# Hybrid decoder layer on one core: output projection with its weight differences in 2 KB buffers, two of the four and the last branch's merge on VectorE, and low parts ordered behind the state additions

## The chip, the core and the metric

The kernel runs on one core of a Trainium2 chip. The core has five engines, each with an instruction queue of its own that is worked off in order: TensorE (PE in the profile; its weight loads are listed as PEld), VectorE (DVE), ScalarE (ACT), GpSimd (POOL) and SyncE (SP). SP does no arithmetic; it issues nearly all DMA transfers. POOL can issue DMAs too, and only there does this kernel use a DMA that adds to its destination. An engine waits on semaphores, so an instruction at the head of a queue that waits holds everything queued behind it.

The metric is the time of one execution on the device, in microseconds (us). Smaller is better. The time before is the median of three runs.

## The reference

One layer of a decoder trunk over 1024 tokens of width 1024, in float32. Three branches (sparse attention, a convolution module, cross-attention into a memory) are projected to the model's width, merged by gates, and sent through one output projection `w_out`. A gated MLP follows.

```python
merged = gm[:, :, 0] * br_nsa + gm[:, :, 1] * br_conv + gm[:, :, 2] * br_mem
h = x + merged @ w_out

hn = rms_norm(h, norm_ffn)
return h + (jax.nn.silu(hn @ w_gate) * (hn @ w_up)) @ w_down
```

Each `gm` is the sigmoid of a projection of the normed input, each `br` a branch times its own output weight (512 by 1024). The change touches the last steps of `merged` and the product `merged @ w_out`, with the addition of `x`.

## The kernel before

**Number format.** A float32 operand of a product is split in a high part (a copy to the type `float32r`) and a low part (the operand minus its high part). A product takes three matmuls per tile of 128 rows: high by high, high by low, low by high. `split` (L134) makes the parts. ScalarE always writes the high part (L135). The low part is a subtraction on VectorE (`sub`, L127; the instruction shows as L128), or on GpSimd when that engine is passed. If `nc.sync` is passed, ScalarE writes minus the high part into the low part's place (L138) and an adding DMA from GpSimd's queue adds the operand (L139).

**Buffers.** `slab` has 16 buffers of 8 KB per partition. Weight parts come from `wsl` (3) and `fsl` (2); `anyslab` deals them out in the fixed turn wsl, wsl, fsl, wsl, fsl. Raw loads land in `st` (2 buffers of 4 KB), `t4` (4 of 4 KB) or `t2` (6 of 2 KB); the profile writes tiles of both `t4` and `t2` as `t`. There are eight PSUM banks of 128x512: three each of two pools, one of a third (all `ps`) and one `pf`.

**The merge (L872 to L912).** Branches are handled in the order convolution, memory, attention (`n_` = 0, 1, 2). Each makes 16 products of 128 channels by 512 tokens, 12 matmuls each. For each 128 channels `d_`, the raw gates are loaded into a `t4` tile `zz` (L883), made a sigmoid by ScalarE (L884), and for each half of the tokens VectorE multiplies PSUM by the gates (L895 for the first branch, L897 for the others). From the second branch on, GpSimd adds the result to the sum in `acc` (L898). In the last branch three of the four quarters of the sum are split at once into `left` (L904; 12 of the 16 products), and `a_sums` (L864) makes four combinations of the quarters on VectorE, one call for each pair of channel groups.

**The output projection (L1042 to L1097).** The product of 1024x1024 by 1024x1024 is made as seven half-size products (a Strassen-Winograd scheme). Products are collected in two sets of four PSUM banks, `X` and `Y`; each is 48 matmuls (`out_product`, L1024, matmuls at L1031). After some of them `into_h` (L1034) adds the banks to the state `H` on VectorE (L1038) and, for a final piece, ScalarE sums its squares (L1040). A product that starts a set anew, or goes on with it, must wait until `into_h` has read the bank. The order is:

1. `X` = `left[0,0]` by `w_1`, where `w_1` is the first quarter B11 of the weight; into H.
2. `Y` = `s_1` by `w_5`, with `w_5` the parts of B12-B11; into H.
3. `X` += `s_2` by `w_6`, with `w_6` the parts of B22-(B12-B11); into H.
4. `Y` += `s_4` by `w_3` (B22), one row tile after the other; into H, final.
5. `Y` = `left[0,1]` by `w_2` (B21), by tile; into H, final.
6. `X` += `s_3` by `w_7` (B22-B12) and `left[1,1]` by `w_4` (B21 minus the difference used for `w_6`), in two groups of two row tiles, each followed by an `into_h` (in `finish`), while the state is normed and transposed for the MLP (L959 to L1012).

The weight differences are kept in `t_`, two `t4` tiles of 128 x 2 x 512, from L910 until `w_4` has been split (L1078); GpSimd works them out at L912, L1052 and L1064, and the ones for `w_7` at L1072. The quarters B11, B22, B21 and the minuend of `w_7` pass through the two `st` buffers one after another, so each load waits for the users of the one before. `w_1`, `w_5`, `w_6` and `w_3` use the adding DMA for their low parts; `w_2`, `w_7` and `w_4` use VectorE.

The state `H` (four slabs of 1 MB) is loaded from `x` by SP at L1045, after the parts of `s_1` in program order.

**What sets the order.** The kernel is written as one stream. The framework puts each engine's instructions in an order when the program is built, by priority in program order and by a simulated timeline of its own (`schedule_with_timeline_sim=True`, L1314). On the chip that order is fixed; what differs from the simulated times becomes waiting. `tc.add_manual_dep` with `ORDER` (L32, used by `behind`, L130) adds an edge that orders two instructions in the queue without a semaphore.

Of the kernel before, what the change touches and what calls it, by code (L numbers as in the profile page):

```python
# [8 lines left out]
F32 = mybir.dt.float32  # L9
# [3 lines left out]
OP = mybir.AluOpType  # L13
# [26 lines left out]
def hybrid_layer_kernel(  # L40
# [4 lines left out]
    nc = tc.nc  # L45
# [40 lines left out]
    def t4(shape, dt=F32):  # L86
        return t4p.tile([P] + shape, dt, tag="t4", name=nm("t4"))

    def t2(shape, dt=F32, p=P):
        return t2p.tile([p] + shape, dt, tag="t2", name=nm("t2"))  # L90
# [34 lines left out]
            tc.cur_priority = self.was  # L125

    def sub(eng, o, a, b):  # L127
        eng.tensor_tensor(o, a, b, op=OP.subtract)  # L128

    def behind(m, before, reason):  # L130
        for b in before or ():
            tc.add_manual_dep(m.ins, b.name, ORDER, reason=reason)

    def split(hi, lo, src, eng=None, after=None):  # L134
        first = nc.scalar.copy(hi, src)  # L135
        behind(first, after, "behind the parts of the rows")
        if eng is nc.sync:
            nc.scalar.activation(lo, hi.bitcast(F32), AF.Copy, scale=-1.0)  # L138
            nc.gpsimd.dma_start(lo, src, accum_op=OP.add)  # L139
        else:  # L140
            sub(eng or nc.vector, lo, src, hi.bitcast(F32))
        return first.ins

    def recip_rms(ss, n, eps, w):
# [191 lines left out]
    sums = []  # L336
# [48 lines left out]
    b = bank([4, TAPS + 3])  # L385
# [5 lines left out]
    b = bank([2, 16])  # L391
# [45 lines left out]
    b = bank([NT, 24])  # L437
# [75 lines left out]
    for hp in range(2):  # L513
# [3 lines left out]
        b = bank([2, 256])  # L517
# [3 lines left out]
        hi, lo = (KM[:, hl, 2 * hp:2 * hp + 2, :] for hl in range(2))  # L521
# [90 lines left out]
    with low(TAP):  # L612
        along = products[first_tap:]
        total, run, j = sum(n for _, n in along), 0, 0
# [200 lines left out]
    with low(FILL):  # L815
        for n_ in range(3 * KT):
            b_, d_ = n_ // KT, n_ % KT
            w = w_first if n_ == 0 else col_unit(w_in, C_GM + b_ * D + d_ * P, alloc=fslab,
                                                 eng=nc.sync if n_ > 2 else nc.gpsimd)
            for h_ in range(2):  # L820
                ps = fbank([512])
                for k in range(KT):
                    first = mm3(ps, w[:, 0, k, :], w[:, 1, k, :], xn(0, k, h_), xn(1, k, h_), k == 0, k == KT - 1)
                    j = ((n_ - N_EARLY) * 2 + h_) * KT + k
# [14 lines left out]
    def w_src(kh, dh, j):  # L839
        r0 = (4 * kh + 2 * j) * P  # L840
        return w_out[r0:r0 + 256, halves[dh]].rearrange("(k p) c -> p k c", p=P)

    def w_load(kh, dh, alloc):
        ts = [alloc() for _ in range(2)]
        for j, t in enumerate(ts):
            nc.sync.dma_start(t, w_src(kh, dh, j))
        return ts
# [1 line left out]
    def st2():  # L849
        return stage.tile([P, 2, 512], F32, tag="st", name=nm("st"))  # L850

    def w_parts(ts, eng=None):
        ws = [anyslab([2, 2, 512]) for _ in ts]
        for w, t in zip(ws, ts):
            split(w[:, 0], w[:, 1], t, eng)
        return ws

    def a_parts(th, kh):
        a = [slab([2, 2, 512]) for _ in range(2)]
        for j in range(2):  # L860
            split(a[j][:, 0], a[j][:, 1], merged(th, kh, j))
        return a
# [11 lines left out]
    for n_, (br, src, wt) in enumerate(branches):  # L874
        ins = nxt
        for dp in (range(4) if n_ < 2 else (0, 2, 1, 3)):
            w = unit(wt[0, :, dp * 256:(dp + 1) * 256].rearrange("(k p) c -> p k c", p=P), [4, 256], alloc=anyslab)
            if dp == 2 and n_ < 2:
                nxt = [unit(branches[n_ + 1][1][k], [S], alloc=slab) for k in range(4)]
            for d_ in (2 * dp, 2 * dp + 1):  # L880
                wc = (d_ % 2) * P
                zz = t4([S])
                nc.sync.dma_start(zz, zd[br, d_])  # L883
                nc.scalar.activation(zz, zz, AF.Sigmoid)  # L884
                for half in range(2):
                    z = zz[:, half * 512:(half + 1) * 512]
                    ps = anybank([512])
                    for k in range(4):
                        i_ = ins[k]
                        mm3(ps, w[:, 0, k, wc:wc + P], w[:, 1, k, wc:wc + P],  # L890
                            i_[:, 0, half * 512:(half + 1) * 512], i_[:, 1, half * 512:(half + 1) * 512],
                            k == 0, k == 3)
                    a = acc[dp][:, d_ % 2, half * 512:(half + 1) * 512]
                    if n_ == 0:
                        nc.vector.tensor_tensor(a, ps, z, op=OP.mult)  # L895
                    else:
                        nc.vector.tensor_tensor(z, ps, z, op=OP.mult)  # L897
                        nc.gpsimd.tensor_tensor(a, a, z, op=OP.add)  # L898
                    if n_ == 2 and (half, dp // 2) != (1, 0):
                        m = left.setdefault((half, dp // 2), [None, None])  # L900
                        if d_ % 2 == 0:
                            m[dp % 2] = slab([2, 2, 512])
                        m = m[dp % 2]
                        split(m[:, 0, d_ % 2, :], m[:, 1, d_ % 2, :], a)  # L904
            if n_ == 2 and dp > 1:
                a_sums(dp - 2)
            if n_ == 2 and dp == 1:
                b11 = w_load(0, 0, st2)
                w_1 = w_parts(b11, nc.sync)
                t_ = w_load(0, 1, lambda: t4([2, 512]))  # L910
                for t, b in zip(t_, b11):
                    sub(nc.gpsimd, t, t, b)  # L912

    hd = drp.tile([4, P, 2, D], F32, tag="hd", name="hd")
    FH = FF // P // 2
# [118 lines left out]
    def into_h(B, th, dh, final, ts=range(4)):  # L1034
        for t in ts:
            tp, tt = 2 * th + t // 2, t % 2
            h = H[tp][:, tt, cols[dh]]
            nc.vector.tensor_tensor(h, B[t], h, op=OP.add)  # L1038
            if final:
                nc.scalar.activation(junk, h, AF.Square, accum_out=sq4[tp][:, 2 * tt + dh:2 * tt + dh + 1])  # L1040

    s_1 = a_parts(1, 1)  # L1042
    for tp in range(4):
        H[tp] = slab([2, D], F32)
        nc.sync.dma_start(H[tp], x[tp * 256:(tp + 1) * 256, :].rearrange("(t p) d -> p t d", p=P))  # L1045
    w_5 = w_parts(t_, nc.sync)
    out_product(X, left[0, 0], w_1, True)
    into_h(X, 0, 0, False)
    s_2 = a_parts(0, 0)
    b22 = w_load(1, 1, st2)  # L1050
    for t, b in zip(t_, b22):
        sub(nc.gpsimd, t, b, t)  # L1052
    w_6 = w_parts(t_, nc.sync)
    out_product(Y, s_1, w_5, True)
    into_h(Y, 1, 1, False)
    s_4 = a_parts(0, 1)
    w_3 = w_parts(b22, nc.sync)
    out_product(X, s_2, w_6, False)
    into_h(X, 0, 1, False)
    s_3 = a_parts(1, 0)  # L1060
    b21 = w_load(1, 0, st2)
    w_2 = w_parts(b21)
    for t, b in zip(t_, b21):
        sub(nc.gpsimd, t, b, t)  # L1064
    out_product(Y, s_4, w_3, False, by_tile=True)
    into_h(Y, 0, 1, True)
    w_7 = []
    for j in range(2):
        t, b = st2(), t4([2, 512])
        nc.sync.dma_start(t, w_src(1, 1, j))  # L1070
        nc.sync.dma_start(b, w_src(0, 1, j))
        sub(nc.gpsimd, t, t, b)  # L1072
        w_7 += w_parts([t])
    out_product(Y, left[0, 1], w_2, True, by_tile=True)
    into_h(Y, 0, 0, True)
    for tp in range(2):
        nc.sync.dma_start(hd[tp], H[tp])
    w_4 = w_parts(t_)  # L1078
    def finish(tp, a, w, dh):
        ts = range(2 * (tp - 2), 2 * (tp - 1))  # L1080
        out_product(X, a, w, False, by_tile=True, ts=ts)
# [88 lines left out]
    w = pieces(1)  # L1170
# [147 lines left out]
```

## Time and profile before

| | |
|---|---|
| time, median of 3 runs | 1721.66 us (1720.76 to 1721.7) |
| time of the profiled execution | 1721.86 us |
| span in its profile | 1720.2 us, 24513 instructions |
| busy: PE, DVE, ACT, POOL | 98%, 61%, 46%, 34% |
| mean granted TensorE clock | 0.995 |

The profiled execution lies 1.66 us above its span: that is what lies around the span. Start times in the profile are microseconds from the span's start. A row of the timeline gives start, length, engine, line, operation, output and input tiles and the count of merged instructions; in brackets stands idle time of the engine before it and what ended it. The last products of the merge run on PE until about 984 us, the output projection from there to about 1096 us, and the MLP from there to the end.

### The profile page before, as it was taken

What the parts mean: (1) busy time and instruction counts of PE and PEld (TensorE: products, weight loads), DVE (VectorE), ACT (ScalarE), POOL (GpSimd) and SP (SyncE); (2) the same over time, 40 slices, a digit from 0 to 9 for tenths busy, and PEclk for the clock granted to TensorE, in tenths of its full rate; (3) what the DMA queues carried; (4) which work ended last, traced back from release to release, by engine and by line L of the source; (5) the groups of instructions that cost most, each with busy time, mean ns of one, the idle gap of its engine ahead of it and who ended that gap; (6) DMA issues with size and microseconds to landing.
All of it is one profiled execution on the core that took longest, in us unless ns stands there. A gap on an engine that the chain in (4) does not pass through costs nothing.

```text
span 1720.2 us, 24513 instructions
## 1 busy us (share of the span) xinstructions
PE 1686.9 (98%) x9050; PEld 1452.6 (84%) x9050; DVE 1051.3 (61%) x1773; ACT 789.0 (46%) x1427; POOL 588.6 (34%) x549
## 2 busy tenths in 40 slices
PE   7999999999999999999999988999999999999999
PEld 7887898999888889989888877888888888888887
DVE  5399798644355456766754677865455544457655
ACT  6413655534476566766654345532222232233332
POOL 1101012323254334343205731665565777310000
PEclk9999999999999999999999999999999999999999
DMA  6435445243233322121475563232333454794663
GB/s 198 108 79 153 121 123 125 61 106 99 74 92 88 91 69 59 50 70 57 131 249 195 141 202 135 80 123 90 113 98 116 147 166 165 266 374 155 227 233 122
DMA packets 180673, 230.12 MB, mean 134 GB/s; under 512 B 11382, under 2 KB 118056, under 8 KB 179530
## 3 DMA queue, kind: packets, MB, share of 16 engines
q1 hardware_dynamic: 173786, 203.92, 35.7%
q0 software_dynamic: 6768, 24.64, 7.6%
q8 instruction: 71, 1.16, 0.3%
q14 instruction: 48, 0.39, 0.1%
HBM read 153.55 MB, written 50.33 MB: 119 GB/s over the span
## 4 chain that ended last, share of the span: by engine, by line
PE 90%; DMA 3%; ACT 2%; DVE 2%; issue 1%; POOL 1%; SPq 0%; POOLq 0%; DVEq 0%; ACTq 0%
PE ps L154 52%; PE pf L154 18%; PE ps L1252 11%; PE ps L776 3%; PE ps L1031 2%; PE pf L1252 1%; DMA st<-in_w_out_dram 1%; DMA wsl<-st 1%; PE ps L220 1%; POOL t L128 0%; POOL slab L898 0%; ACT slab L135 0%; DMA t<-in_w_out_dram 0%; DMA wsl<-in_cmp_w_dram 0%; PE ps L702 0%
## 5 line engine op out<-in xcount | busy, mean ns | idle before, releaser
L154 PE MATMUL ps<-slab,wsl 128*128 128x512 f32 (+1 forms) x1616 | 360.5, 381 | 0.4 <-DMA wsl<-in_cmp_w_dram 0.4
L154 PEld LDWEIGHTS ps<-slab,wsl 128*128 128x128 f32 x1616 | 293.4, 188 | 58.4 <-issue 0.5
L154 PE MATMUL pf<-slab,fsl 128*128 128x512 f32 x1236 | 327.0, 401 | 3.9 <-ACT fz L828 3.8
L154 PEld LDWEIGHTS pf<-slab,fsl 128*128 128x128 f32 x1236 | 223.5, 189 | 44.9 <-ACT fz L828 5.3
L154 PE MATMUL ps<-wsl,slab 128*128 128x256 f32 x1344 | 173.2, 285 | 0.3 <-DVE slab L229 0.2
L154 PEld LDWEIGHTS ps<-wsl,slab 128*128 128x128 f32 x1344 | 167.4, 192 | 3.1 <-issue 1.0
L1150 DVE TENSOR_TENSOR t<-ps,t 128x512 f32<-128x512 f32 x127 | 86.8, 687 | 120.2 <-PE ps L154 119.4
L154 PE MATMUL ps<-slab,fsl 128*128 128x512 f32 x684 | 159.5, 389 | 0.0
L404 DVE SCALAR_TENSOR_TENSOR slab<-slab,cw 128x1021 f32<-128x1021 f32 (+15 forms) x120 | 156.0, 1303 | 2.2
L154 PEld LDWEIGHTS ps<-slab,fsl 128*128 128x128 f32 x684 | 128.4, 188 | 26.7
L128 DVE TENSOR_TENSOR t<-ps,t 128x512 fp32r<-128x512 f32 (+3 forms) x195 | 119.5, 630 | 31.6 <-ACT t L135 30.2
L135 ACT CAST t<-ps 128x512 fp32r<-128x512 f32 (+2 forms) x192 | 98.1, 539 | 44.5 <-PE ps L776 34.9
L1252 PE MATMUL ps<-wsl 128*128 128x512 f32 x492 | 117.7, 389 | 0.0
L154 PE MATMUL ps<-t,slab 128*128 128x256 f32 x624 | 116.4, 291 | 1.2 <-DVE t L128 1.2
L1252 PEld LDWEIGHTS ps<-wsl 128*128 128x128 f32 x492 | 92.3, 188 | 19.2
L135 ACT CAST wsl<-st 128x1024 fp32r<-128x1024 f32 x64 | 67.2, 1050 | 80.1 <-PE ps L154 34.5
L154 PEld LDWEIGHTS ps<-t,slab 128*128 128x128 f32 x624 | 94.2, 189 | 7.6 <-DVE t L128 1.6
L154 PE MATMUL ps<-slab,qt 128*128 128x384 f32 (+3 forms) x384 | 95.2, 339 | 1.0 <-DVE sm L744 1.0
L135 ACT CAST wsl<-t 128x1024 fp32r<-128x1024 f32 x45 | 47.4, 1054 | 96.5 <-POOL t L128 32.9
L690 POOL TENSOR_SCALAR wsl<-wsl,sm,gsb 128x640 f32<-128x640 f32 (+7 forms) x76 | 59.0, 791 | 87.0 <-DVE sm L685 82.7
L1252 PE MATMUL ps<-fsl 128*128 128x512 f32 x333 | 80.5, 389 | 0.0
L1163 POOL TENSOR_TENSOR t<-t,t 128x512 f32<-128x512 f32 x21 | 40.2, 1913 | 116.8 <-DVE t L1150 53.7
(256 smaller groups left out, 2858.8 us busy)
## 6 DMA issues: line engine op xcount, KB each, us to landing
t<-in_w_down_dram SPq DMA_DIRECT2D x70, 256.0 KB, 3.7
fst<-in_w_in_dram SPq DMA_DIRECT2D x24, 512.0 KB, 4.5
zd<-fz SPq DMA_DIRECT2D x48, 256.0 KB, 2.3
t<-zd SPq DMA_DIRECT2D x24, 512.0 KB, 4.7
st<-in_w_in_dram SPq DMA_DIRECT2D x22, 512.0 KB, 4.7
st<-in_w_gate_dram SPq DMA_DIRECT2D x22, 512.0 KB, 3.9
st<-in_w_up_dram SPq DMA_DIRECT2D x22, 512.0 KB, 4.1
ad<-t SPq DMA_DIRECT2D x44, 256.0 KB, 2.7
```

Source lines behind the costliest of these rows:

```text
L128: eng.tensor_tensor(o, a, b, op=OP.subtract)
L135: first = nc.scalar.copy(hi, src)
L154: m = nc.tensor.matmul(o, a, b, start=start, stop=stop)
L220: m = nc.tensor.transpose(b[:, kk, tt * P:(tt + 1) * P], js[tt][:, k * P:(k + 1) * P], ident)
L404: return nc.vector.scalar_tensor_tensor(acc[:, s:], u[:, :S - s], cw[:, ct, 30 - s:31 - s], acc[:, s:], op0=OP.mult, op1=OP.add)
L690: nc.gpsimd.tensor_scalar(tiles[h], tiles[h], rec[:, h:h + 1], gsb[:, i, c0:c0 + 1], op0=OP.mult, op1=OP.mult)
L776: nc.tensor.transpose(b[:, j - j0, h, :], tiles[h][:, j * P:(j + 1) * P], ident)
L1031: nc.tensor.matmul(B[t], a_, b_, start=start and k == 0 and j == 0, stop=k == 3 and j == 2, skip_group_check=True)
L1150: nc.vector.tensor_tensor(o, a_, b_, op=OP.add)
L1163: nc.gpsimd.tensor_tensor(u4, u4, c22, op=OP.mult)
L1252: nc.tensor.matmul(B[t], a_, b_, start=start and k == 0 and j == 0, stop=k == FH - 1 and j == 2, skip_group_check=True)
```

## The change

The diff is shown whole but for the context that it leaves alone.

- `split` and `w_parts` take `low_after`: instructions behind which the low part's subtraction is ordered on its engine. `into_h` returns its last addition for this. So `w_2`'s low parts are ordered behind the additions of product 3, `w_7`'s behind those of product 4, `w_4`'s behind those of product 5.
- `t_` becomes four `t2` tiles of 128x512 instead of two `t4` tiles of 128x1024. It is loaded by four DMAs instead of two, and its parts for `w_5`, `w_6` and `w_4` are made in pieces of 512 columns: twice the ScalarE instructions, and twice the adding DMAs or VectorE subtractions, each half as wide. `w_sums` makes the differences in the same pieces.
- The differences at L1064 and L1072 (for `w_4` and `w_7`) go from GpSimd to VectorE; those at L912 and L1052 (for `w_5` and `w_6`) stay on GpSimd.
- The additions at L898 go to VectorE in the last branch.
- The loads of `H[0]` and `H[1]` stand ahead of `s_1`'s parts in the program.

```diff
     def sub(eng, o, a, b):
-        eng.tensor_tensor(o, a, b, op=OP.subtract)
+        return eng.tensor_tensor(o, a, b, op=OP.subtract)
...
-    def split(hi, lo, src, eng=None, after=None):
+    def split(hi, lo, src, eng=None, after=None, low_after=None):
...
-            sub(eng or nc.vector, lo, src, hi.bitcast(F32))
+            behind(sub(eng or nc.vector, lo, src, hi.bitcast(F32)), low_after, "behind the sums of the blocks before")
...
-    def w_parts(ts, eng=None):
+    def w_parts(ts, eng=None, low_after=None):
         ws = [anyslab([2, 2, 512]) for _ in ts]
         for w, t in zip(ws, ts):
-            split(w[:, 0], w[:, 1], t, eng)
+            if isinstance(t, list):
+                for k in range(2):
+                    split(w[:, 0, k], w[:, 1, k], t[k], eng, low_after=low_after)
+            else:
+                split(w[:, 0], w[:, 1], t, eng, low_after=low_after)
         return ws
+
+    def w_sums(eng, ts, bs, a_first):
+        for t, b in zip(ts, bs):
+            for k in range(2):
+                sub(eng, t[k], *((t[k], b[:, k]) if a_first else (b[:, k], t[k])))
...
-                        nc.gpsimd.tensor_tensor(a, a, z, op=OP.add)
+                        (nc.gpsimd if n_ == 1 else nc.vector).tensor_tensor(a, a, z, op=OP.add)
...
-                t_ = w_load(0, 1, lambda: t4([2, 512]))
-                for t, b in zip(t_, b11):
-                    sub(nc.gpsimd, t, t, b)
+                t_ = [[t2([512]) for _ in range(2)] for _ in range(2)]
+                for j in range(2):
+                    for k in range(2):
+                        nc.sync.dma_start(t_[j][k], w_src(0, 1, j)[:, k])
+                w_sums(nc.gpsimd, t_, b11, True)
...
-            nc.vector.tensor_tensor(h, B[t], h, op=OP.add)
+            m = nc.vector.tensor_tensor(h, B[t], h, op=OP.add)
...
-
-    s_1 = a_parts(1, 1)
-    for tp in range(4):
+        return [m.ins]
+
+    def residual(tp):
         H[tp] = slab([2, D], F32)
         nc.sync.dma_start(H[tp], x[tp * 256:(tp + 1) * 256, :].rearrange("(t p) d -> p t d", p=P))
+
+    residual(0)
+    residual(1)
+    s_1 = a_parts(1, 1)
+    residual(2)
+    residual(3)
     w_5 = w_parts(t_, nc.sync)
...
-    for t, b in zip(t_, b22):
-        sub(nc.gpsimd, t, b, t)
+    w_sums(nc.gpsimd, t_, b22, False)
...
-    into_h(X, 0, 1, False)
+    done = into_h(X, 0, 1, False)
     s_3 = a_parts(1, 0)
     b21 = w_load(1, 0, st2)
-    w_2 = w_parts(b21)
-    for t, b in zip(t_, b21):
-        sub(nc.gpsimd, t, b, t)
+    w_2 = w_parts(b21, None, done)
+    w_sums(nc.vector, t_, b21, False)
     out_product(Y, s_4, w_3, False, by_tile=True)
-    into_h(Y, 0, 1, True)
+    done = into_h(Y, 0, 1, True)
...
-        sub(nc.gpsimd, t, t, b)
-        w_7 += w_parts([t])
+        sub(nc.vector, t, t, b)
+        w_7 += w_parts([t], None, done)
     out_product(Y, left[0, 1], w_2, True, by_tile=True)
-    into_h(Y, 0, 0, True)
+    done = into_h(Y, 0, 0, True)
     for tp in range(2):
         nc.sync.dma_start(hd[tp], H[tp])
-    w_4 = w_parts(t_)
+    w_4 = w_parts(t_, None, done)
+
```

## The prediction

> **What bounds the kernel now.** I read the page first: the busy shares and the chain of work that ended last.
>
> ```profile
> PE 1686.9 (98%) x9050; PEld 1452.6 (84%) x9050; DVE 1051.3 (61%) x1773; ACT 789.0 (46%) x1427; POOL 588.6 (34%) x549
> ...
> PE 90%; DMA 3%; ACT 2%; DVE 2%; issue 1%; POOL 1%; SPq 0%; POOLq 0%; DVEq 0%; ACTq 0%
> ```
>
> PE is the bound, so a change off PE can win only what PE loses in gaps. Second, the table of stretches from the last branch on (length; busy time of PE, PEld, DVE, ACT, POOL with instruction counts; granted clock; DMA share; GB/s).
>
> ```profile
> 940.00:984.25 44.25, 44.25 (x196) 36.62 (x196) 29.06 (x28) 17.08 (x20) 29.14 (x19) 1.00 0.49 142
> 990.50:995.50 5.00, 0.04 (x1) 0.00 (x0) 4.80 (x4) 2.93 (x3) 4.07 (x2) 0.93 0.25 94
> 995.50:998.25 2.75, 2.73 (x7) 2.15 (x8) 1.45 (x2) 1.24 (x2) 2.53 (x3) 0.50 0.02 6
> 998.25:1005.10 6.85, 6.85 (x24) 5.46 (x23) 6.78 (x7) 5.20 (x6) 0.85 (x1) 0.75 0.95 248
> 1035.90:1041.70 5.80, 0.00 (x0) 0.00 (x0) 3.11 (x3) 1.10 (x2) 3.92 (x2) 0.78 0.03 12
> 1041.70:1052.10 10.40, 10.34 (x37) 8.41 (x38) 5.51 (x8) 7.23 (x15) 0.00 (x0) 0.79 0.46 150
> 1130.00:1500.00 370.00, 370.00 (x1634) 306.35 (x1634) 190.15 (x215) 107.29 (x136) 229.49 (x152) 1.00 0.43 141
> ```
>
> PE stands still in two stretches, and runs at 0.50 to 0.79 of its clock behind them. The MLP row shows PE busy for all of 370 us: what is won before it should reach the end. Third, PE's own timeline gives the gaps exactly.
>
> ```profile
> 984.25 4.02 PE L1031 MATMUL ps<-wsl,slab 128*128 128x512 f32 x17
> 988.11 2.43 PE L1031 MATMUL ps<-fsl,slab 128*128 128x512 f32 x10
> 995.52 2.93 PE L1031 MATMUL ps<-wsl,slab 128*128 128x512 f32 x6 [4.98 <-DVE t L897]
> 998.25 7.02 PE L1031 MATMUL ps<-fsl,slab 128*128 128x512 f32 x23
> ...
> 1013.94 5.60 PE L1031 MATMUL ps<-wsl,slab 128*128 128x512 f32 x24
> 1019.38 5.60 PE L1031 MATMUL ps<-fsl,slab 128*128 128x512 f32 x24
> ...
> 1034.34 1.52 PE L1031 MATMUL pf<-fsl,slab 128*128 128x512 f32 x6
> 1041.76 10.43 PE L1031 MATMUL ps<-wsl,slab 128*128 128x512 f32 x36 [5.90 <-DVE slab L1038]
> ```
>
> Undisturbed, 24 matmuls take 1019.38 - 1013.94 = 5.44 us, 0.2267 each. **Gap A**, inside product 1: 4.98 us idle; then 6 matmuls in 2.73 instead of 1.36 us and 23 in 6.85 instead of 5.21. That is 4.98 + 1.37 + 1.64 = 8.0 us. **Gap B**, ahead of product 5: 5.90 us idle, then 36 matmuls in about 10.3 instead of 8.2: 8.0 us. Together 16.0 us. Fourth, the chain and VectorE's timeline tell who is late.
>
> ```profile
> 982.98 1.72 POOL slab L898
> 984.71 4.11 DMA t<-zd
> 988.91 1.06 ACT t L884
> 991.45 3.41 DVE slab L128
> 994.86 0.61 DVE t L897
> ...
> 1031.30 3.58 DMA st<-in_w_out_dram
> 1035.13 2.35 POOL st L128
> 1037.51 1.05 ACT fsl L135
> ```
>
> ```profile
> 1038.59 2.42 DVE L128 TENSOR_TENSOR fsl<-st,fsl 128x1024 fp32r<-128x1024 f32 x1 [3.83 <-ACT fsl L135]
> 1040.93 1.87 DVE L1038 TENSOR_TENSOR slab<-ps,slab 128x512 f32<-128x512 f32 x3
> ```
>
> A: the last gates could be loaded only when a POOL addition had freed a `t4` buffer (`t_` holds two of four). Then load, sigmoid, a low part lengthened to 3.41 us, and the multiplication that frees the bank product 1 needs. B: VectorE stands at the low part of `w_7`, which waits for load, POOL difference and high part; the state additions of product 4, whose four tiles of 12 matmuls were finished from 1027.5 to 1035.7 (1034.34 + 6 x 0.2267, and 2.72 between tiles), are queued behind it, and PE waits for the first.
>
> Behind the idle stretches the granted clock stood at 0.50 and 0.75, and at 0.79; that cost 3.0 and 2.1 us beyond the idle time. The Trainium skill, "TensorE: Matmul & The Clock Gate", section "What's actually happening", says that an idle window of about 3.4 us halves the clock until a busy one has passed; by that an estimate of 1.7 us goes with each gap, and the two would be worth 14.3 us. The trace agrees on the half clock and shows more loss; the measured loss stands in my sum.
>
> **The change part by part.** Prices, from groups of 940 to 1000 us (VectorE's from 940 to 985), the timelines of VectorE, POOL and SP, one line's view, the DMA issues of 930 to 1030 us and the waits of 984 to 1096 us:
>
> ```profile
> L128 DVE TENSOR_TENSOR slab<-slab,slab 128x512 fp32r<-128x512 f32 x8 | 12.9, 1618 | 6.0 <-ACT slab L135 6.0
> 954.03 0.69 DVE L128 TENSOR_TENSOR slab<-slab,slab 128x512 fp32r<-128x512 f32 x1 [1.75 <-ACT slab L135]
> L867 DVE TENSOR_TENSOR slab<-slab,slab x2: 1207/1216/1225, 969.4 to 998.6; 128x1024 f32<-128x1024 f32 x2
> L898 POOL TENSOR_TENSOR slab<-slab,t 128x512 f32<-128x512 f32 x18 | 27.2, 1555 | 9.3 <-DVE t L897 9.3
> L128 POOL TENSOR_TENSOR t<-st,t 128x1024 f32<-128x1024 f32 x2 | 5.7, 2872 | 3.4 <-DMA wsl<-t 3.4
> L139 POOL DMA_DIRECT2D fsl<-t x1 | 0.9, 865 | 0.0
> L135 ACT CAST slab<-slab 128x512 fp32r<-128x512 f32 x12 | 7.4, 614 | 16.1 <-POOL slab L898 16.1
> L135 ACT CAST wsl<-t 128x1024 fp32r<-128x1024 f32 x2 | 2.1, 1044 | 3.7 <-POOL t L128 3.7
> 1007.42 0.87 POOL L139 DMA_DIRECT2D fsl<-t  x1 [2.35 <-ACT fsl L138]
> 971.73 2.62 SPq L846 DMA_DIRECT2D st<-in_w_out_dram  x2
> fsl<-t POOLq DMA_DIRECT2D x2, 512.0 KB, 7.9
> st<-in_w_out_dram SPq DMA_DIRECT2D x4, 512.0 KB, 4.0
> DVE slab L1038 <- DMA slab<-in_x_dram: 9.2, 4, 4.0
> ```
>
> *`t_` in `t2`.* The gates get all four `t4` buffers back, so the last two loads wait for the fifth and sixth group instead of the last but one: they move some 15 us forward, and the chain of A loses its DMA and sigmoid. `t_` has no user before it in `t2`, and is free again (after `w_4`) well before the MLP's norms want those buffers.
>
> *Pieces of 512.* Each pair of ScalarE casts costs 2 x 0.614 - 1.044 = 0.18 us more, under 4 us in all on an engine with half its time free. The adding DMAs for `w_5` and `w_6` become eight of 256 KB: four more issues of 0.87 us on POOL, hidden because POOL loses its additions. No row has an adding DMA of 256 KB; a pair takes between 7.9 us (as one of 512 KB) and 15.8 (each like one of 512 KB). I take 7.9, since pieces share one queue and the same bytes. `w_6`'s second half decides: it waits for product 1 to free its buffer, and is due 1.5 products (16.3 us) after that. Before, the issue at 1007.42 came 4.4 us after product 1's end (the last 9 of the 23 matmuls belong to product 2, so 1003.0); with the longer casts, a second issue and the DMA that is 4.4 + 1.3 + 7.9 = 13.6, or 21.5: in time, or 5.2 late. Cost 0, upper end +5.2.
>
> *Sixteen additions to VectorE.* Nearest row: a low part of the same shape with both inputs in SBUF, 0.69 alone, 1.618 mean beside POOL. So 11.0 to 25.9 us on VectorE, in a stretch of 44.25 us of which 29.06 are busy. I take 0.69 plus a share. The eight low parts hold 12.9 - 8 x 0.69 = 7.4 us of waiting beside POOL, some 9 with `a_sums`; POOL's 27.2 us of additions largely leave, differences of about 11 us stay, so of these 9 some 2.4 remain. VectorE: 29.1 - 9 + 2.4 + 11 = 33.5 of 44.25. It keeps up.
>
> *The handover after 984.25.* VectorE must finish the last product's multiplication and addition (0.68 + 0.69), up to four low parts (2.8), four `a_sums` (4.9) and two low parts of `s_1` (2.4): 11.5 us, while product 1 holds PE for 47 x 0.2267 = 10.7 (one of its 48 runs earlier). I charge 1.0 us, so A gives 7.0 of 8.0.
>
> *Differences for `w_4`, `w_7` to VectorE; low parts behind additions.* About 4 x 0.69 + 2 x 1.22 = 5.2 us join VectorE, where the queue stood idle 3.83 us and waited 9.2 us for `H`. POOL's 2.35 to 2.87 each leave the weight chain. A new wait: `w_2`'s low parts stand behind product 3's additions, and the release of `st` and `w_7`'s load behind them. From the middle of product 2: 19.0 us to those additions' end, 2.4 low parts, 2.8 differences, 4.0 load, then difference, high part and low part twice, about 6: 34.2. `w_7` is due after 0.5 + 3 products, 38.1. Slack 4; I charge 0.8 for what the built order may add. `w_4`'s low parts wait for product 5's last addition, and are due 24 matmuls (5.4 us) later; four of 0.69 fit. So B gives 7.2.
>
> *`H` earlier.* Two of the four loads get the two slabs that are free, ahead of the crowded time; with products 8 us earlier, the 9.2 us that the additions waited for `x` would otherwise grow. I cost it at nothing; if it fails, those 9.2 us stand ahead of products 3 and 4. The other two wait for the merge's last operands, until 984.25, and hold what SP queues behind them. If that is B22's loads (at 971.73 before), `w_6`'s first half has 984.3 + 4.0 load + 2.9 difference + 2 casts + 1.7 issues + 7.9 = 1002.8, before product 3's start at 984.25 + 10.7 + 10.9 = 1005.8: hidden.
>
> Sum: 7.0 + 7.2 = 14.2 us. The profiled execution took 1721.86 us (span 1720.2), 0.2 above the median, so 1707.7, or **1707.5 us** against the median.
>
> **The rivals.**
>
> *Only one gap closes.* For it: the planner set VectorE's order in B wrongly, and may do so again with a new difference waiting for a load ahead of product 4's additions; or the 5.2 us above come true. Against: `w_7`'s load can't start before product 3's additions. One gap of 8.0 us gone, none to 2 us of the other: 1711.5 to 1716.5, middle 1713.7.
>
> *It doesn't do what it says.* The gates come early, but the weights of products 3 to 6 were the true limit, a DMA after a DMA in the chain. Then PE waits at a weight for as long: 1718 to 1721.9, about 1720. Against: the slacks of 3 and 4 us above.
>
> *Slower: VectorE late at the handover.* If an addition costs c, VectorE ends 29.06 + 16c - 44.25 us late at 984.25. The bank came free at 994.86 + 0.61 = 995.5 before, 11.2 us after its product. A is as long as now when 16c = 26.4, c = 1.65; the measured mean beside POOL is 1.618. With c = 1.9 A grows by 4.0 us, and with B left the result is 1726. For it: the row of 1618 ns. Against: 0.69 alone, and POOL's additions are the neighbour that goes. The Trainium skill's rule on this, "SBUF — State Buffer", section "SBUF: two separate sides": VectorE with two SBUF inputs and GpSimd take a shared port pair in turns, each for a whole instruction. By that rule the additions lose time to the differences that stay on POOL; the trace's 1618 beside 690 agrees.
>
> **How the numbers follow.** Both gaps close: 0.60 (1703.5 to 1711.5; the low end takes all 16.0 us and two more for small waits that I haven't priced). One closes: 0.22. Nothing: 0.09. Slower: 0.09. The range to leave out no more than 0.2: 1703.5 to 1716.5, which takes in the 5.2 us of the DMAs. A measurement of this kernel tells about 0.2% (3.4 us) from no change: faster 0.82, same 0.09, slower 0.09.
>
> **What would show it.** PE's timeline: no idle over 1 us between the merge and product 6, granted clock 1.00 throughout, products 10.9 us apart. The last gates loaded before 970 us; L898 on VectorE at about 0.7 us; L1038 never idle for `x`. Wrong if additions run over 1.6 us, if PE's wait names an adding DMA or a `wsl`/`fsl` low part, or if VectorE waits for `st` ahead of L1038.

## The result and the profile after

| | before | after |
|---|---|---|
| median | 1721.68 us of 4 runs | 1711.17 us of 4 runs (1710.08 to 1712.12) |
| ratio, 95% interval | | 0.994 (0.9923 to 0.9957) |
| profiled execution, its span | 1721.86, 1720.2 us | 1711.06, 1709.3 us |

The change makes the kernel 10.5 us faster; 14.2 were forecast. The page's busy times of the kernel after (engine, us, share of the span, instructions):

```profile
PE 1684.6 (99%) x9050; PEld 1451.4 (85%) x9050; DVE 1052.9 (62%) x1797; ACT 789.7 (46%) x1437; POOL 559.4 (33%) x537
```

The stretches of the kernel after, in the columns of the prediction's table: product 1 with its operands, product 5, the norms' set-up, the MLP.

```profile
981.70:1000.00 18.30, 17.16 (x76) 13.86 (x75) 17.37 (x22) 11.66 (x18) 5.59 (x5) 1.00 0.89 301
1028.30:1039.30 11.00, 11.00 (x50) 9.09 (x49) 7.58 (x11) 7.41 (x15) 0.00 (x0) 1.00 0.56 191
1055.00:1100.00 45.00, 42.01 (x196) 34.72 (x195) 37.26 (x51) 26.96 (x50) 21.65 (x14) 0.92 0.21 73
1120.00:1480.00 360.00, 360.00 (x1590) 298.08 (x1589) 186.10 (x210) 103.65 (x132) 226.54 (x149) 1.00 0.42 135
```

The clock is 1.00 in all of these but the third. PE's timeline of the kernel after shows where it still stands:

```profile
983.42 4.24 PE L1042 MATMUL ps<-wsl,slab 128*128 128x512 f32 x18
...
990.17 1.67 PE L1042 MATMUL ps<-wsl,slab 128*128 128x512 f32 x6 [1.15 <-DVE t L906]
...
1027.06 1.52 PE L1042 MATMUL pf<-fsl,slab 128*128 128x512 f32 x6
1028.42 8.32 PE L1042 MATMUL ps<-wsl,slab 128*128 128x512 f32 x36
...
1078.69 1.20 PE L992 MATMUL ps<-ident,t 128*128 128x128 f32 x9 [0.77 <-DVE t L976]
1082.11 1.12 PE L992 MATMUL ps<-ident,t 128*128 128x128 f32 x4 [2.22 <-DVE t L960]
...
1083.45 5.22 PE L154 MATMUL ps<-slab,fsl 128*128 128x512 f32 x13
```

The lines are 9 to 16 further down than before: L906 multiplies a product of the merge by its gate, L907 adds, L1042 is the output projection, L1049 adds into the state, L992 transposes for the norms.

**Gap A** shrank. Four products of 48 matmuls at 0.2267 us take 43.5 us undisturbed. From the merge's end to product 4's end it was 1035.70 - 984.25 = 51.45 us before and 1028.42 - 983.42 = 45.00 after: 7.9 us lost before, 1.5 after. **Gap B** is gone: product 5 starts at 1028.42, straight behind product 4 (1027.06 and six matmuls), and its 36 matmuls take 8.2 us instead of 10.3. That is 6.06 us between the products and 2.1 of slow clock, 8.1 in all. **A third gap grew**, ahead of the MLP; call it C. Before, PE stood there once, at full clock:

```profile
1095.51 0.66 PE L981 MATMUL ps<-ident,t 128*128 128x128 f32 x4 [1.17 <-DVE t L949]
...
1096.23 3.15 PE L154 MATMUL ps<-slab,fsl 128*128 128x512 f32 x13
```

After, it stands 0.77 + 2.22 = 2.99 us, 1.8 more, and what stands behind it runs slower: the 13 matmuls take 5.22 us instead of 3.15, and from the start of the last four transposes to the end of the 13 it is 6.56 us instead of 3.87. That is 2.7 us of slow clock (0.50 to 0.56 was granted from 1082.10 to 1088.50), so C costs 4.5 in all. The merge's end came 0.8 us earlier too (984.25 - 983.42); it lies between 981.6 and 984.4 in the profiles of this document, so this is no gain of the change that can be told from scatter. So 6.5 + 8.1 + 0.8 - 4.5 = 10.9, which is what the spans differ by.

### The profile page after: what moved, and what is told of

Same layout as the page of the kernel before. It is cut to its first block, busy times and chain, and to the rows that moved or that the text cites. A ratio compares the mean times of both kernels' runs of the same rounds, so it can differ in the third digit from the quotient of the medians.

```text
span 1709.3 us, 24524 instructions
## 1 busy us (share of the span) xinstructions
PE 1684.6 (99%) x9050; PEld 1451.4 (85%) x9050; DVE 1052.9 (62%) x1797; ACT 789.7 (46%) x1437; POOL 559.4 (33%) x537
## 5 line engine op out<-in xcount | busy, mean ns | idle before, releaser
L128 DVE TENSOR_TENSOR t<-ps,t 128x512 fp32r<-128x512 f32 (+3 forms) x195 | 119.5, 630 | 30.0 <-ACT t L135 28.5
L135 ACT CAST wsl<-t 128x1024 fp32r<-128x1024 f32 (+1 forms) x48 | 47.7, 1000 | 92.8 <-POOL t L128 27.8
```

The costliest lines, as they stand in the source:

```text
L128: return eng.tensor_tensor(o, a, b, op=OP.subtract)
```

## The experiments

Two theories stood at first. By the prediction's, the gates' buffers close A, and the order of the low parts closes B. By its rival, GpSimd's additions were what held the merge back, the buffers do little, and differences on VectorE with earlier loads close B. What grew in C was open. Eleven kernels were run, one of them twice. Those called "before and" add one or two parts of the change to the kernel before, the others take parts out of the changed kernel. Later expectations call the two theories by letters: G (gates) and V (VectorE's additions) for A, O (order), D (differences) and E (earlier loads or buffers) for B. The loss in A is the time from the merge's end to product 4's end, less 43.5 us, worked out as above from each run's timeline; C is PE's idle time on the last transposes ahead of the MLP. Each comes from one profile, and the loss in A moves by several us for the same work. Up to product 1's end b_low has the instructions of the kernel before in the same order, and loses 2.5 us there instead of 8.0; its other 2.5 us lie in product 3, at an addition into the state and an adding DMA. After, v_root, u_low4 and u_low4_r have one order there too, and lose 1.5 to 4.5 us. In all kernels but b_low the whole of A lies in product 1.

| kernel | A lost | idle ahead of product 5 | C idle | time, us |
|---|---|---|---|---|
| before | 7.9 | 5.90 | 1.17 | 1721.7 |
| after | 1.5 | 0 | 2.99 | 1711.17 (4 runs) |
| after, a late copy moved (v_root) | 4.5 | 0 | 2.99 | 1710.2 (5 runs) |
| after, without `w_4`'s order (u_low4) | 4.3 | 0 | 1.17 | 1707.43 |
| the same again (u_low4_r) | 3.9 | 0 | 1.17 | 1709.81 (5 runs) |
| after, without any order (u_low) | 6.0 | 0 | 1.17 | 1711.72 |
| and the differences on GpSimd (u_lowsubs) | 5.2 | 0 | 1.36 | 1709.83 |
| after, additions on GpSimd (u_merge) | 20 | 0 | 3.01 | 1728.24 |
| after, `t_` in two `t4` (u_t4) | 1.2 | 0 | 2.22 | 1709.11 |
| before and additions on VectorE (b_merge) | 1.7 | 8.35 | 1.17 | 1716.02 |
| before and `t2` buffers (b_t2) | 20 | 0 | 1.17 | 1724.12 |
| before and the orders (b_low) | 5.0 (2.5 in product 1) | 0 | 1.48 | 1712.4 |
| before and additions, two orders (b_min) | 1.7 | 0.29 | 1.43 | 1709.23 (5 runs) |
| u_low4 and gates first on SP (u_gate) | 0.8 | 0 | 1.18 | 1706.61 (5 runs) |

### Where the third gap came from

First, one copy on ScalarE that stood ahead of the last norm's root was ordered behind it:

```diff
+    for o, b in last_copy:
+        behind(nc.scalar.copy(o, b), [roots[-1]], "behind the last root")
```

> The changed kernel with one edit: of the four ScalarE copies of the third group's transposes, the one into the second fz buffer is ordered behind the last square root (L146) in ScalarE's queue. Queue theory (the new gap at 1078 to 1082 us comes from ScalarE: the last square root, ready at 1070.5, ran at 1073.6 behind a copy that waited 1.4 us for GpSimd): the root runs about 2.3 us earlier, the two waits of 0.77 and 2.22 us shrink to under 1 us in all, the slow clock behind them (2.1 us) goes, time about 1707. Rival (VectorE's amount of work between product 5 and the norms is the limit, whatever the order): the same 53.6 us from product 5's start to the end of the wait, time 1711 within 1 us.

ScalarE's timeline of the kernel after, and of this run, both ahead of the last root (L146):

```profile
1071.61 0.59 ACT L1006 COPY fz<-ps 128x512 f32<-128x512 f32 x1 [1.39 <-POOL t L128]
1072.09 1.14 ACT L135 CAST slab<-t 128x512 fp32r<-128x512 f32 x2
...
1073.61 0.21 ACT L146 ACTIVATE sm<-sm 128x2 f32<-128x2 f32 x1
```

```profile
1074.95 1.14 ACT L135 CAST slab<-t 128x512 fp32r<-128x512 f32 x2 [1.39 <-POOL t L128]
...
1076.47 0.21 ACT L146 ACTIVATE sm<-sm 128x2 f32<-128x2 f32 x1
```

The copy left, and the same 1.39 us for GpSimd stands ahead of the two casts. C did not change; the ratio was 0.9942 (0.9929 to 0.9956). The single copy was not the cause. Next the orders were taken out, first `w_4`'s alone, then all three:

```diff
-    w_4 = w_parts(t_, None, done)
+    w_4 = w_parts(t_)
```

> The changed kernel without the order for w_4's low parts alone. If that order is what makes VectorE late for the norms (they ran at 1040.9 to 1043.4 in the stretch where it is fullest): the waits at 1078 to 1082 fall to about 1.2 us as before the change, time 1707 to 1708. If the queue of ScalarE is the cause: the waits stay at 3 us, time 1711 within 1 us.

> The changed kernel without any of the three orders for low parts. If the order closed gap B: product 5 stands still for 4 to 6 us again and time goes to 1717 to 1719. If the differences on VectorE and the earlier loads closed it: w_7's first low part stands ahead of product 4's additions, but its inputs come early enough for a wait of at most 2 us ahead of product 5, time at most 1713.

Both have C back at 1.17 us without slow clock behind it, the first although its loss in A was larger than the changed kernel's. Every other kernel of the table without `w_4`'s order has 1.17 to 1.43. With it stand 2.22 to 3.01 us, and 1.48 in b_low, where the differences for `w_4` are still GpSimd's. So `w_4`'s order makes C longer by 1.8 us in the changed kernel.

What the orders cost behind product 5's start is seen more fully in the time from there to the end of the span, slow clock included. The five changed kernels without `w_4`'s order take 676.1 to 676.5 us; the four with it take 680.9 (after), 679.5, 679.6 and 678.3. The kernel before and b_merge take as long as the former, once product 5's own slow clock (2.1 and 2.6 us) is taken off, b_t2 677.3. But on the kernel before the orders cost there too: b_low takes 680.3, and b_min 680.7 with no order for `w_4` at all. Their waits stand earlier in the norms' set-up, where the table's column for C does not show them (b_low's 2.39 us and b_min's 1.17 below). So leaving out `w_4`'s order is what helps in the changed kernel; on the kernel before, the orders for `w_2` and `w_7` are enough to bring the loss.

PE's, ScalarE's and VectorE's timelines of u_low4, at the same place; the root stands directly behind its input there, while after, the root at 1073.61 came 3.1 us behind the reduction (1070.35 and 0.14):

```profile
1081.19 0.66 PE L992 MATMUL ps<-ident,t 128*128 128x128 f32 x4 [1.17 <-DVE t L960]
```

```profile
1073.12 0.25 ACT L146 ACTIVATE sm<-sm 128x2 f32<-128x2 f32 x1
```

```profile
1072.82 0.16 DVE L972 TENSOR_REDUCE sm<-sm 128x2 f32<-128x4 f32 x1 [0.22 <-ACT junk L1051]
```

The order shifted instructions on three engines behind product 5. Which of these shifts does it is open; the one copy is ruled out.

u_low brought a second finding: without any order there was no wait ahead of product 5 either.

### What closed gap A

The changed kernel with one line undone:

```diff
-                        (nc.gpsimd if n_ == 1 else nc.vector).tensor_tensor(a, a, z, op=OP.add)
+                        nc.gpsimd.tensor_tensor(a, a, z, op=OP.add)
```

> The changed kernel with the last branch's additions back on GpSimd. If the two freed t4 buffers closed gap A: the last gates are still loaded by 970, product 1 waits at most 2 us, time within 1.5 us of 1711. If the additions on VectorE closed it (0.69 instead of 1.55 us each, and no lock-step with GpSimd): the multiplications are late again, product 1 waits 3 us or more and the clock falls, time 1715 to 1718.

It is slower than before, and by far slower than either theory expected; why is seen in b_t2 below. Then each part by itself on the kernel before: this line put in, and the buffers alone.

> The kernel before with one part of the change alone: the last branch's additions on VectorE. Theory V (the additions close gap A, the idle inside the first product; gap B, ahead of the fifth, has another cause): gap A falls from 8.0 us with its slow clock to some 1 to 3, gap B stays at about 8 in all or less where the products reach it later; time 1713.5 to 1717. Theory G (the last gates' buffers close gap A, the additions do not): the last gates are loaded after 970 as before, gap A stays at 5 or more, time 1719 to 1723.

> The kernel before with the 2 KB buffers alone; the additions and all differences stay on GpSimd. Theory V: the gates come earlier, but GpSimd's additions still set the end of the last branch, so gap A does not shrink and may grow as it did with the additions given back (three idles of 3.22, 3.67 and 8.49 us); gap B stays; time 1720 to 1730. Theory G: gap A closes by some 6 us; time 1713 to 1717.

b_t2 has the change's lines for `t_` and `w_sums`, with all differences left on GpSimd. PE's and then ScalarE's timeline of b_merge (L884 is the sigmoid of a gate there):

```profile
988.88 1.67 PE L1031 MATMUL ps<-wsl,slab 128*128 128x512 f32 x6 [1.33 <-DVE t L897]
...
1035.49 10.91 PE L1031 MATMUL ps<-wsl,slab 128*128 128x512 f32 x36 [8.35 <-DVE slab L1038]
```

```profile
983.10 1.06 ACT L884 ACTIVATE t<-t 128x1024 f32<-128x1024 f32 x1 [1.29 <-DMA t<-zd]
```

PE's, ScalarE's and GpSimd's timelines of b_t2:

```profile
984.61 0.96 PE L1042 MATMUL ps<-wsl,slab 128*128 128x512 f32 x3 [2.79 <-DVE t L906]
989.25 5.42 PE L1042 MATMUL ps<-wsl,slab 128*128 128x512 f32 x15 [3.67 <-DVE t L906]
...
1004.50 2.92 PE L1042 MATMUL ps<-wsl,slab 128*128 128x512 f32 x6 [8.25 <-DVE t L906]
```

```profile
974.48 1.06 ACT L893 ACTIVATE t<-t 128x1024 f32<-128x1024 f32 x1
...
999.57 1.57 ACT L135 CAST slab<-slab 128x512 fp32r<-128x512 f32 x2 [7.47 <-POOL slab L907]
```

```profile
997.06 1.26 POOL L128 TENSOR_TENSOR t<-st,t 128x512 f32<-128x512 f32 x1 [5.61 <-DMA wsl<-t]
998.28 1.26 POOL L907 TENSOR_TENSOR slab<-slab,t 128x512 f32<-128x512 f32 x1
```

Theory V holds on both sides. In b_merge the last gates are still late (983.10), and A is 1.7 us. They are 5.8 us earlier than before, though (3.3 counted from the merge's end), with the same buffers: the load of the last gates waits for an addition to free its buffer, and the additions are done sooner. And VectorE waited for no gate there; it has no idle time from 979.75 to 990.0. The kernel won less than A gave, because PE came earlier to product 5 and gap B grew, to 8.35 us idle. In b_t2 gap B, which was expected to stay, is gone, since PE comes to product 5 9.4 us later than before (1045.07 against 1035.70). The last sigmoid of b_t2 starts at 974.48, nothing waits for a gate from there on, and PE stands 14.7 us: a difference on GpSimd waits 5.61 us for an adding DMA, the merge's addition stands behind it, ScalarE's cast waits 7.47 us for that, and VectorE behind the cast. With the additions on VectorE there is no GpSimd queue between the merge and product 1. The changed kernel with `t_` back in 4 KB buffers says the same from the other side:

```diff
-                t_ = [[t2([512]) for _ in range(2)] for _ in range(2)]
+                t_ = [[q[:, k] for k in range(2)] for q in (t4([2, 512]), t4([2, 512]))]
```

> The changed kernel with the four 2 KB buffers given back: t_ again lies in two 4 KB buffers. Theory V: gap A stays within 3 us, because the additions are still VectorE's; time 1709 to 1713. Theory G: the last two gates are loaded late again, gap A comes back with 5 to 8 us, time 1715 to 1719.

A lost 1.2 us there, with the last gate's sigmoid at 986.30. The three profiles with the additions on VectorE and `t_` in 4 KB buffers lose 1.2 to 1.7 us in A, the six with 2 KB buffers 1.5 to 6.0 (without u_gate, below). The buffers are not what won A. How much the additions won is less sure. With 2 KB buffers it is far beyond the scatter: 20 us in A and 1728.24 us with them on GpSimd. With 4 KB buffers the two profiles with them on GpSimd lose 8.0 and 2.5 us in product 1, the three with them on VectorE 1.2 to 1.7, and b_merge's one run (1716.02) lies 1.9 us under the fastest of 23 runs of the kernel before (1717.9).

### What closed gap B

> The kernel before with the orders alone (low parts of w_2, w_7 and w_4 behind the state's additions). Theory O (the order closes gap B): no idle and no slow clock around the fifth product's start, gap A as before, and w_4's order adds up to 4 us ahead of the MLP; time 1713 to 1718. Theory D (gap B closes because the differences leave GpSimd or start earlier, the order adds nothing): gap B stays at 5 us or more, and w_4's order comes on top; time 1721 to 1726.

The edit, on the kernel before:

```diff
-    w_2 = w_parts(b21)
+    w_2 = w_parts(b21, None, done)
...
-        w_7 += w_parts([t])
+        w_7 += w_parts([t], None, done)
...
-    w_4 = w_parts(t_)
+    w_4 = w_parts(t_, None, done)
```

VectorE's timeline of b_low (L1038 adds into the state there):

```profile
1024.80 2.47 DVE L1038 TENSOR_TENSOR slab<-ps,slab 128x512 f32<-128x512 f32 x4
1027.20 2.34 DVE L128 TENSOR_TENSOR wsl<-st,wsl 128x1024 fp32r<-128x1024 f32 x2
1029.46 1.87 DVE L1038 TENSOR_TENSOR slab<-ps,slab 128x512 f32<-128x512 f32 x3
...
1035.92 2.33 DVE L128 TENSOR_TENSOR fsl<-st,fsl 128x1024 fp32r<-128x1024 f32 x1 [3.98 <-ACT fsl L135]
```

VectorE still stands 3.98 us for `w_7`'s first part, but now behind product 4's four additions (the last of them at 1031.26), and PE doesn't feel it: product 5 follows product 4 without a wait. So theory O holds, and the order is enough. The time, 1712.4 us, is 0.6 under the range of that theory, and it has part of its gain from A, where the work in product 1 was the same. PE's timeline of b_low, and then product 5's start in b_min, which is b_merge with the orders for `w_2` and `w_7`:

```profile
990.36 1.67 PE L1031 MATMUL ps<-wsl,slab 128*128 128x512 f32 x6 [2.18 <-DVE t L897]
...
1014.61 5.08 PE L1031 MATMUL ps<-fsl,slab 128*128 128x512 f32 x21 [1.60 <-DMA fsl<-t]
...
1051.27 1.63 PE L1031 MATMUL ps<-fsl,slab 128*128 128x512 f32 x6 [2.39 <-DVE sm L961]
```

```profile
1027.32 8.45 PE L1031 MATMUL ps<-wsl,slab 128*128 128x512 f32 x36 [0.29 <-DVE slab L1038]
...
1048.18 1.63 PE L1031 MATMUL ps<-fsl,slab 128*128 128x512 f32 x6 [1.17 <-DVE sm L961]
```

b_merge and b_min together show the order most clearly: PE is done with product 4 at 1026.98 in b_merge and at 1026.86 in b_min, and the wait ahead of product 5 falls from 8.35 us to 0.29. Why did u_low do without? The differences were put back on GpSimd as well:

```diff
-    w_sums(nc.vector, t_, b21, False)
+    w_sums(nc.gpsimd, t_, b21, False)
...
-        sub(nc.vector, t, t, b)
+        sub(nc.gpsimd, t, t, b)
```

> The changed kernel without the three orders, and with the differences for w_4 and w_7 back on GpSimd: only the additions, the buffers and the place of the loads of H are left of the change. Theory D (with no order, gap B was closed by the differences' move to VectorE): the wait for L1049 ahead of the fifth product comes back with 5 to 8 us; time 1713 to 1719. Theory E (the buffers or the earlier loads of H close B, the differences' engine does not matter): B stays closed, gap A 1 to 3 us, time 1707 to 1712.

VectorE's timelines of u_lowsubs and of b_merge, where the same low part (L128) stands ahead of the additions:

```profile
1029.64 1.23 DVE L128 TENSOR_TENSOR fsl<-st,fsl 128x1024 fp32r<-128x1024 f32 x1 [2.24 <-ACT fsl L135]
1030.78 1.88 DVE L1049 TENSOR_TENSOR slab<-ps,slab 128x512 f32<-128x512 f32 x3
```

```profile
1032.47 2.27 DVE L128 TENSOR_TENSOR fsl<-st,fsl 128x1024 fp32r<-128x1024 f32 x1 [3.89 <-ACT fsl L135]
1034.66 1.87 DVE L1038 TENSOR_TENSOR slab<-ps,slab 128x512 f32<-128x512 f32 x3
```

By its time theory E holds and D falls, though A lost more than either expected. But it holds with nothing to spare. The additions come 3.9 us earlier in u_lowsubs, by its buffers or its earlier loads, which weren't told apart. PE reaches product 5 4.5 us later (1031.53 against 1026.98, product 4's ends): its merge ended 1.0 us later, and A lost 5.2 us instead of 1.7. The first addition was done at 1031.4, when PE arrived. In b_merge the additions came 7.7 us behind PE (1034.66 - 1026.98); so about half of that was taken up by an earlier chain, and half by a later PE. By these figures an estimate of some 4 us of B would be left by an earlier chain alone if A were closed; no run shows it. u_low stands in the same place: its PE was done with product 4 only at 1033.91. So the order closes B, but that the changed kernel needs it is not shown. The order leaves nothing.

### What is enough, and what more there is to win

Three kernels with five runs each: the two parts that the above leaves as causes, put on the kernel before (b_merge's line, and `done` for `w_2` and `w_7`); u_low4 again; and u_low4 with one more order, since SP's queue in the changed kernel held two gate loads behind a load that waited for a buffer.

```diff
-    b22 = w_load(1, 1, st2)
+    b22 = w_load(1, 1, st2, [gate])
```

where `gate` is the last load of a gate, and the loads of `b22` are ordered behind it.

> The kernel before with two parts alone: the last branch's additions on VectorE, and w_2's and w_7's low parts behind the state's additions; no 2 KB buffers, no difference moved, no order on w_4. If these two are what the gain comes from: gap A about 1.3 us as in the run of the additions alone, gap B gone, 1.17 us ahead of the MLP; time 1705.5 to 1708.5, below the changed kernel. If the buffers and the moved differences are needed as well: 1710 to 1716.

> The changed kernel without w_4's order, again and in rounds. If w_4's order costs what the one profile showed (1.8 us of idle and 2.1 us of slow clock ahead of the MLP, against gap A, which differs from run to run by 1 to 3 us): median 1706 to 1709, ratio to before 0.991 to 0.993. If the one run was luck: 1710 to 1712, ratio 0.994.

> The same, and on SyncE's queue the loads of B22 stand behind the last branch's last gate. If the two gate loads held behind B22's first load (which waits for a buffer until 951.5) are what leaves 1.2 to 2.7 us of gap A: gap A falls below 1 us and the median is 1 to 3 us under the kernel without this edge, 1704 to 1707. If the backlog of VectorE has another cause: gap A stays, the time is the same within 1 us, or up to 3 us more, because B22 lands later and the third and fourth products wait for its parts.

b_min has a ratio of 0.9931 (0.9917 to 0.9944) and 1709.23 us; its five runs lie within 0.6 us. That is 0.7 us above the range expected if the two parts make the gain, and below the other. They are enough for all that the change brings, but five small waits of 0.24 to 1.17 us came up between product 4's end and the MLP, beside C's 1.43, that u_low4 has not; with them the way from product 5 to the end takes 4.5 us longer than u_low4's, as said above. u_low4_r has 0.9932 (0.992 to 0.9945), 1709.81 us with runs from 1707.05 to 1711.18, between its two expectations. By the intervals neither can be told from the other or from the changed kernel, though u_low4_r's median stands 1.4 us below the latter, the way C says. That is far less than C's 4.5 us. Its profile lost 2.4 us more in A than that of the kernel after, so what leaving out `w_4`'s order is worth in time is not settled. u_gate has 0.9918 (0.9903 to 0.9933), 1706.61 us, the best median of all; its interval overlaps those of the kernel after and of u_low4_r, its runs but for one lie under all of the kernel after. SP's and then VectorE's timeline of the kernel after, and the same of u_gate:

```profile
951.46 0.38 SPq L846 DMA_DIRECT2D st<-in_w_out_dram  x1
951.94 1.49 SPq L892 DMA_DIRECT2D t<-zd  x2
```

```profile
958.65 1.23 DVE L128 TENSOR_TENSOR wsl<-st,wsl 128x1024 fp32r<-128x1024 f32 x1 [5.57 <-ACT wsl L135]
```

```profile
938.53 25.78 SPq L892 DMA_DIRECT2D t<-zd  x6
964.40 0.90 SPq L846 DMA_DIRECT2D st<-in_w_out_dram  x2
```

```profile
954.63 1.23 DVE L128 TENSOR_TENSOR wsl<-st,wsl 128x1024 fp32r<-128x1024 f32 x1 [2.02 <-ACT wsl L135]
```

All gates go out ahead of the load of `b22`. The cast that VectorE waits for stands on ScalarE behind a sigmoid; it comes earlier, the wait falls from 5.57 to 2.02 us, and A's last idle time from 1.15 to 0.41. The profiled run of u_gate, the fastest of its five, has a mean clock of 1.000. Its runs still spread from 1703.78 to 1710.16; where the slower ones lose their time wasn't seen, since each kernel has one profile.

## Why the prediction was right, and where it was not

- **What bounds the kernel.** Right. PE's idle time and its slow clock explain the difference of the spans, and the MLP row passed everything on: PE is busy for all of 360 us after, as it was before. But the norms' set-up lies between the last product and the MLP, and that stretch did not pass it on: C's 4.5 us are a little more than what the forecast had too much (14.2 - 10.5 = 3.7); B, 0.9 better than forecast, made up for some of it.
- **`t_` in `t2`: "the chain of A loses its DMA and sigmoid".** It did, as forecast: the last sigmoid starts at 970.48 instead of 988.91. But that was not the limit. ScalarE's row after:

```profile
970.48 1.06 ACT L893 ACTIVATE t<-t 128x1024 f32<-128x1024 f32 x1 [0.43 <-DMA t<-zd]
```

b_t2 has early gates and a longer A, b_merge late gates and a short one. The row read for it, a load 4.11 us long in the chain of waits, was the last link of a queue whose start was GpSimd's additions.
- **"Sixteen additions to VectorE".** The cost was right: the group took 12.0 us, 754 ns each, between the 11.0 and the 25.9 of the bounds.

```profile
L907 DVE TENSOR_TENSOR slab<-slab,t 128x512 f32<-128x512 f32 x16 | 12.0, 754 | 0.2
```

It was put on the wrong side of the sum: it is the part that won A, 6.5 of the forecast 7.0 us. That the number for A came out is luck: the step it was worked out from, the buffers, gives no faster kernel by itself (b_t2, 1724.12 us), and the change happened to hold the part that does it.
- **The handover.** 1.0 us was charged, 1.5 measured. VectorE's wait of 5.57 us some 25 us earlier, behind SP's queue, may be part of it: u_gate lost 0.8. But A moves by more than that from one profile to the next, so the share is not settled.
- **Pieces of 512.** Taken at nothing, and PE waited for no part of `w_5` or `w_6`. The upper end of 5.2 us wasn't touched.
- **Low parts behind additions.** The step for B was right and worth 8.1 instead of 7.2; b_min beside b_merge and b_low show the order alone, on the kernel before. `w_4`'s share of that sentence, "four of 0.69 fit", is the step that failed: the low parts were never late for PE themselves, but work of the norms moved with them, and C grew by 1.8 us of idle time and 2.7 of slow clock. Which of the moved instructions does it stays open.
- **`H` earlier.** The loads are earlier, but not as was said: all four go out in one stretch, none ahead of the others. The row of SP's timeline of the kernel after:

```profile
982.32 2.22 SPq L1056 DMA_DIRECT2D slab<-in_x_dram  x4
```

Before it was 997.69, and no addition waits for `x` any more. What the loads' place is worth by itself was not tried.
- **The rivals.** None came. VectorE late at the handover would have needed 1.65 us per addition. Nearest to the measured time was "only one gap closes" (from 1711.5), for another reason: both gaps closed, and a third took back 4.5 of the 14.6 us that they gave.

## What to carry to other kernels

The last link of a chain of waits (a DMA, a sigmoid) can be late only because a queue ahead of it is; price the removal of each link alone before believing that one of them is the limit. When work is ordered behind an addition, its own due time is not enough: look at what the planner will place in the stretch where it goes, up to the next point at which PE waits. And loads that can go at once may stand ahead of those that wait for a buffer on the same queue; here that cut VectorE's wait, and the time fell, though not by more than the intervals leave open.

## What the runs showed of the hardware

The loss by slow clock does not follow from the length of an idle stretch. Four kernels stand the same 2.2 us at C. PE's timelines of v_root and of u_t4, to be set beside that of the kernel after:

```profile
1085.46 1.11 PE L992 MATMUL ps<-ident,t 128*128 128x128 f32 x4 [2.21 <-DVE t L960]
...
1086.80 3.86 PE L154 MATMUL ps<-slab,fsl 128*128 128x512 f32 x13
```

```profile
1082.88 0.66 PE L992 MATMUL ps<-ident,t 128*128 128x128 f32 x4 [2.22 <-DVE t L960]
...
1083.60 3.15 PE L154 MATMUL ps<-slab,fsl 128*128 128x512 f32 x13
```

The 13 matmuls take 5.22 us in the kernel after, 3.86 in v_root, 3.96 in u_merge and 3.15 in u_t4: 2.1, 0.7, 0.8 and no us lost in them. The first three have another idle stretch of 0.8 us that ended 3.4 us before this one did, u_t4 has not. In gap A the longer stretch was the cheaper one; PE's timelines of u_low4 and u_low4_r, six matmuls each:

```profile
989.86 2.93 PE L1042 MATMUL ps<-wsl,slab 128*128 128x512 f32 x6 [2.54 <-DVE t L906]
```

```profile
990.97 1.65 PE L1042 MATMUL ps<-wsl,slab 128*128 128x512 f32 x6 [2.75 <-DVE t L906]
```

The granted clock was 0.50 over u_low4's six (989.86 to 992.58), and 1.00 over those of u_low4_r.

The Trainium skill, "TensorE: Matmul & The Clock Gate", section "What's actually happening", says that the monitor's window of about 3.4 us runs freely, so that the point of change depends on where in it the work falls; the differing losses agree with that. It also says that the slow clock comes after a whole idle window; u_low4's 2.54 us of idle time were enough, so the trace does not bear this out.
